# Memory's keys and half of its values projected at the start of a two-block kernel

## The chip, the cores and the metric

The kernel runs on one core of a Trainium2 chip. Its engines are TensorE (PE, with PEld for its weight loads), VectorE (DVE), ScalarE (ACT), GpSimd (POOL) and SyncE (SP); each has its own queue of instructions, and SP and POOL also issue DMA transfers. The metric is the device time of one execution in microseconds (us), less is better. Times are the median of several runs. The profile belongs to one further execution, and its span is the time inside it that the trace covers.

## The reference, cut to what matters

A first block (rmsnorm, an input projection `w_in`, a convolution, gated linear attention, a lookup over 128 x 128 experts) works on 16 meta tokens and 256 tokens of width 2048. A second block takes its 256 tokens and mixes a DeltaNet branch with cross attention to a memory. The memory's keys and values depend on inputs alone, on nothing that the first block computes:

```python
def second_block(x, mem, norm_g, mem_norm_g, mem_w_kv, ...):
    mem_n = rms_norm(mem, mem_norm_g)              # mem: 256 x 2048
    ...
        xa = memory_cross_attention(xq, mem_n, mem_w_kv[i], ...)

def memory_cross_attention(xq, mem_n, w_kv, qn_g, kn_g):
    q = rms_norm(xq.reshape(B, S, XA_HEADS, XA_DIM), qn_g)
    kv = jnp.einsum("bmd,de->bme", mem_n, w_kv)    # w_kv: 2048 x 2048
    k = rms_norm(kv[..., :XA_WIDTH].reshape(B, -1, XA_HEADS, XA_DIM), kn_g)
    v = kv[..., XA_WIDTH:].reshape(B, -1, XA_HEADS, XA_DIM)
    ...
```

The experts' output of the first block is a sum over chosen rows of a value table: `sum_k w[k] * V[idx[k]]`.

## The kernel before

Every product of fp32 matrices is made as three matmuls of parts (`mm3`, L203 to L213): an operand is cast into a `hi` part (ScalarE, L176) and a `lo` part that holds the rest (VectorE, L177), and L206, L207 and L208 multiply hi by hi, and each hi by the other's lo. Weights stream in by `load` (L185, issued on SP) as blocks of 1 MB in one of RW = 4 buffers `raw`; `halved` makes of each two halves `hi` and `lo` (HL = 4 buffers each). `proj_a` projects tokens against 512 columns: 4 loads, and for each load 24 matmuls, 96 in a block of 512 columns.

At the start SP issues `meta`, the two tiles of `x` (L111, L114) and eight small rows of gains (`prows`, L155), which TensorE turns into `prm`. Then comes the first norm: squares of the three tiles (`junk`, ScalarE L263), a row of factors made on TensorE (`along`, L297, L298), and for each of 16 slices three transposes (TensorE, L335), a product with the factors (`xs`, VectorE L337) and the split into `xh` and `xl` (L179, L180). The first projection of `w_in` follows.

The memory comes late. `memory` (a generator in `Background`, which the helpers advance by a rate at each tick) loads the memory in both layouts, makes the gain-weighted features `mh` and `ml` (L179 and L180 at its call) and the row factors `mr` (squares at L904) while TensorE works in the loop over hidden experts (L753, L754). Behind this loop stands a branch (L1141) whose body is a fallback for many chosen experts; POOL and SP wait there for a count. Behind the branch `weigh` (L1047) makes weights of pairs of experts: four gathers on POOL into `gq` and `hq` (two buffers each), their product `hq` (VectorE, L1062) and its split into `wh` and `wl` (seven buffers). Five pairs are weighed ahead (WA = 5). Then all four blocks of `w_kv` are projected (two of keys, two of values; 384 matmuls), with norms of the keys (`heads_norm`), their transposes (L318) and stores into `kmd` and `vmd`. The value loop follows: per pair of experts two gathers of 1 MB rows of V on POOL (`v_row` into `raw`), the split, 48 matmuls of 512 columns, and one `weigh` five pairs ahead, for 47 pairs.

The order of the instructions on each engine is set by a scheduler of the framework from a model of their durations; from the expert block on, that of TensorE is the order of the program.

Of the kernel before, what the change touches and what calls it, by code (L numbers as in the profile page):

```python
# [18 lines left out]
D = 2048  # L19
# [55 lines left out]
def _build(tc, nc, V, S, T, G, ctx, I, out):  # L75
# [31 lines left out]

    pn1 = ctx.enter_context(ExitStack())
    nw1 = pn1.enter_context(pool("norm1"))
    meta = nw1.tile([NM, D], F32, name="meta", bufs=1)  # L110
    nc.sync.dma_start(meta, I["meta_tokens"])  # L111
    h = hp.tile([128, 2, D], F32, name="h")
    for t in range(2):
        nc.sync.dma_start(h[:, t], I["x"][0, t * 128:(t + 1) * 128, :])  # L114
# [212 lines left out]

    w_in = I["w_in"][0]
    xh, xl = x_tiles(NM + NT)
    toks = [(meta, NM, 0), (h[:, 0], 128, NM), (h[:, 1], 128, NM + 128)]  # L330
    rB = along(nw1, rstd_of(square_sums(toks, nw1.tile([128, D], F32, name="junk")), D, [128, 3]), toks)
    for k in range(KT):
        p = (acc, ptp, acc, pmm)[k % 4]()
        for x, n, o in toks:
            T.transpose(p[:, o:o + n], chunk(x, k), ident[:n, :n])  # L335
        xs = nw1.tile([128, NM + NT], F32, name="xs", bufs=3)
        V.tensor_mul(xs, p[:, :NM + NT], rB)  # L337
        split_store(xh[:, k], xl[:, k], xs, pcol(N1, k))
# [551 lines left out]

    kmd = tc.dram_tile([128, 8, 256], F32, name="kmd")
    vmd = tc.dram_tile([128, 2, 1024], F32, name="vmd")
    def memory():

        ss = me.tile([128, 2, 4], F32, name="ssq")
        for hf in range(2):
            raw = load(I["mem_T"][:, hf * 8:hf * 8 + 8], [8, NT])
            for k in range(8):
                split_store(mh[:, hf * 8 + k], ml[:, hf * 8 + k], raw[:, k], pcol(MG, hf * 8 + k))
                yield  # L900
        for t in range(2):
            x = load(I["mem_2"][0, t * 128:(t + 1) * 128, :], [D])
            for q in range(4):
                S.activation(acc(), x[:, q * 512:(q + 1) * 512], AF.Square, accum_out=ss[:, t, q:q + 1])  # L904
            yield
        s1 = me.tile([128, 2], F32, name="ssr")
        V.tensor_reduce(s1, ss, axis=AX.X, op=OP.add)
        V.tensor_copy(mr, rstd_of(s1, D, [128, 2]))
        yield

# [210 lines left out]
    for e2 in range(NR // 2):  # L1121
        if e2 == MEM:
            pme = ctx.enter_context(ExitStack())
            me = pme.enter_context(pool("mem", side="right"))
            mh = me.tile([128, KT, NT], F32R, name="mh")
            ml = me.tile([128, KT, NT], F32R, name="ml")
            mr = me.tile([128, 2], F32, name="mr")
            bg.add(memory(), 0.75)
        for _ in hidden(e2):
            bg.tick()  # L1130
        if e2 == IX:
            bg.drain()
            index_rows()
# [16 lines left out]
    ws = [weigh(e2, wp, ww) for e2 in range(WA)]  # L1150
    wkv = I["mem_w_kv_2"][0]
    with pool("kvw", side="right") as kvw:
        ks = []
        for cb in range(2):
            for t, a in enumerate(proj_a(wkv, 0, KT, cb * 512, mh, ml)):
                ks.append(kvw.tile([128, 512], F32, name="kn", bufs=4))
                heads_norm(kvw, a, ks[-1], mr[:, t:t + 1])
        for cb in range(2):
            for t, a in enumerate(proj_a(wkv, 0, KT, 1024 + cb * 512, mh, ml)):
                vm2 = kvw.tile([128, 512], F32, name="vn")  # L1160
                S.activation(vm2, a, AF.Copy, scale=mr[:, t:t + 1])
                nc.scalar.dma_start(vmd[:, t, cb * 512:(cb + 1) * 512], vm2)
            km = kvw.tile([128, 4, 256], F32, name="kms")
            for _ in heads_T(ks[cb * 2:cb * 2 + 2], km, 0, 2):
                pass
# [613 lines left out]
```

## Time and profile before

| | us |
|---|---|
| median of 3 runs (3482.99 to 3495.45) | 3494.71 |
| the profiled execution, its own time | 3491.37 |
| its span | 3489.4 |
| TensorE busy in it | 3413.1 |

TensorE is busy for 98% of the span, at a mean granted clock of 0.995 of full speed. A row of the timeline gives start and duration in us, the engine (q behind its name for its queue of DMA issues), the line, the operation and the tiles; what stands in brackets is the engine's idle time ahead of it and what ended that. A row with `x6` joins instructions that follow each other.

### The profile page before, as it was taken

The page shows a single profiled execution, that of the slowest core. Times are in us where ns is not written, and L with a number is a line of the kernel's source. Part 1 is how long each engine was busy: PE and PEld are TensorE (multiplying, and loading weights), DVE is VectorE, ACT ScalarE, POOL GpSimd, SP SyncE. Part 2 cuts the span into 40 slices and gives each one's busy share as a digit, 9 for nine tenths or more (in the row PEclk, how much of TensorE's full clock was granted, in tenths as well). Part 3 has the DMA queues.
Part 4 walks back from the last instruction along what each step waited for, and adds up shares of the span by engine and source line. Part 5 has one row for each costly group of instructions (what it writes and reads, how often), then busy time and mean ns, then how long its engine had stood idle before and what let it go on. Part 6 is the DMA issues. An engine that isn't in the chain of part 4 may idle for free. (4 is left out here: it accounts for less than half of the span.)

```text
span 3489.4 us, 50599 instructions
## 1 busy us (share of the span) xinstructions
PE 3413.1 (98%) x19706; PEld 2968.2 (85%) x19706; DVE 2422.6 (69%) x4504; ACT 1661.4 (48%) x2276; POOL 1052.6 (30%) x660
## 2 busy tenths in 40 slices
PE   8999999999999999999998999999999999999999
PEld 7988899888889988888887788777778899999987
DVE  6975569977658998676554555444457788888775
ACT  6444443446445455455443544333347545544443
POOL 0000000000002888888841456666620000000000
PEclk9999999999999999999999999999999999999999
DMA  5544445667675677778765776666665444554443
GB/s 165 169 146 144 145 133 171 216 217 253 229 235 178 182 203 204 210 224 237 209 210 179 256 256 238 212 213 213 227 200 165 145 153 149 164 163 154 154 157 109
DMA packets 347962, 662.06 MB, mean 190 GB/s; under 512 B 56047, under 2 KB 205781, under 8 KB 318002
## 3 DMA queue, kind: packets, MB, share of 16 engines
q1 hardware_dynamic: 256962, 472.68, 40.9%
q0 software_dynamic: 71328, 165.08, 16.6%
q10 hardware_dynamic: 19424, 20.98, 1.7%
q8 instruction: 157, 2.57, 0.3%
q14 instruction: 91, 0.75, 0.1%
HBM read 620.47 MB, written 38.19 MB: 189 GB/s over the span
## 5 line engine op out<-in xcount | busy, mean ns | idle before, releaser
L176 ACT CAST hi<-raw 128x1024 fp32r<-128x1024 f32 x1093 | 1146.0, 1050 | 1510.7 <-PE acc L208 526.0
L177 DVE TENSOR_TENSOR lo<-raw,hi 128x1024 fp32r<-128x1024 f32 x1093 | 1328.0, 1221 | 646.2 <-ACT hi L176 635.4
L753 PE MATMUL acc<-xx,hi 128*128 128x512 f32 x2048 | 723.1, 398 | 0.0
L843 POOL DMA_INDIRECT table<-gts,idx x256 | 595.0, 2324 | 134.2 <-issue 75.9
L754 PE MATMUL acc<-xx,lo 128*128 128x256 f32 x2048 | 573.7, 280 | 0.0
L753 PEld LDWEIGHTS acc<-xx,hi 128*128 128x128 f32 x2048 | 384.5, 188 | 92.1
L754 PEld LDWEIGHTS acc<-xx,lo 128*128 128x128 f32 x2048 | 386.6, 189 | 0.0
L350 POOL DMA_DIRECT2D table<-zero x16 | 18.0, 1128 | 953.0 <-DVE zero L348 953.0
L206 PE MATMUL acc<-xx,hi 128*128 128x256 f32 x1024 | 304.1, 297 | 0.0
L206 PE MATMUL acc<-xh,hi 128*128 128x272 f32 (+1 forms) x1024 | 300.0, 293 | 0.7 <-DVE hg L431 0.7
L208 PE MATMUL acc<-xh,lo 128*128 128x272 f32 (+1 forms) x1024 | 297.1, 290 | 0.0
L207 PE MATMUL acc<-xl,hi 128*128 128x272 f32 (+1 forms) x1024 | 296.7, 290 | 0.0
L207 PE MATMUL acc<-xx,hi 128*128 128x256 f32 x1024 | 289.1, 282 | 0.0
L208 PE MATMUL acc<-xx,lo 128*128 128x256 f32 x1024 | 289.0, 282 | 0.0
L740 POOL DMA_INDIRECT gq<-table,ig x106 | 152.8, 1442 | 252.5 <-DVE hq L1062 116.7
L440 DVE SCALAR_TENSOR_TENSOR h<-hg,cw,h 128x256 f32<-128x256 f32 x480 | 203.4, 478 | 0.0
L1062 DVE TENSOR_TENSOR hq<-hq,gq 128x512 f32<-128x512 f32 x53 | 36.6, 691 | 234.8 <-DMA hq<-hid,ih 231.7
L206 PEld LDWEIGHTS acc<-xh,hi 128*128 128x128 f32 x1024 | 194.2, 190 | 5.2 <-issue 4.9
L207 PEld LDWEIGHTS acc<-xx,hi 128*128 128x128 f32 x1024 | 195.8, 191 | 0.2
L206 PEld LDWEIGHTS acc<-xx,hi 128*128 128x128 f32 x1024 | 195.5, 191 | 0.2
L208 PEld LDWEIGHTS acc<-xx,lo 128*128 128x128 f32 x1024 | 195.2, 191 | 0.0
L207 PEld LDWEIGHTS acc<-xl,hi 128*128 128x128 f32 x1024 | 194.1, 190 | 1.1 <-issue 1.0
(565 smaller groups left out, 6911.9 us busy)
## 6 DMA issues: line engine op xcount, KB each, us to landing
raw<-in_peer_u_dram SPq DMA_DIRECT2D x128, 1024.0 KB
raw<-in_w_in_dram SPq DMA_DIRECT2D x112, 1024.0 KB
raw<-in_dn_w_in_dram SPq DMA_DIRECT2D x88, 1024.0 KB
raw<-in_w_out_dram SPq DMA_DIRECT2D x48, 1024.0 KB
raw<-in_w_gla_out_dram SPq DMA_DIRECT2D x16, 1024.0 KB
table<-zero POOLq DMA_DIRECT2D x16, 1024.0 KB
raw<-in_w_conv_out_dram SPq DMA_DIRECT2D x16, 1024.0 KB
raw<-in_peer_wq_dram SPq DMA_DIRECT2D x16, 1024.0 KB
```

Of the source, the lines that this page charges most:

```text
L176: S.copy(hi, src)
L177: V.tensor_sub(lo, src, hi)
L206: T.matmul(o, lhsT=lh, rhs=rh, start=start, stop=False)
L207: T.matmul(o, lhsT=lh, rhs=rl, start=False, stop=False)
L208: T.matmul(o, lhsT=ll, rhs=rh, start=False, stop=stop)
L350: nc.gpsimd.dma_start(table[:128 * 128 * NT].rearrange("(q p a b) o -> q p a (b o)", q=16, p=128, b=128)[q], z[:, None, :].to_broadcast([1 ...
L440: V.scalar_tensor_tensor(ca[:, f], hg[:, f - f0, j:j + NT], w, ca[:, f], op0=OP.mult, op1=OP.add)
L740: G.indirect_dma_start(out=dst, out_offset=None, in_=rows, in_offset=bass.IndirectOffsetOnAxis(ap=ids.bitcast(U32), axis=0))
L753: T.matmul(a, lhsT=hi[:, kk], rhs=xxu[:, k].rearrange("p a t -> p (a t)"), start=k == 0, stop=False)
L754: T.matmul(a[:, :NT], lhsT=lo[:, kk], rhs=xh[:, k], start=False, stop=k == KT - 1)
L843: d = G.indirect_dma_start(out=table, out_offset=bass.IndirectOffsetOnAxis(ap=idx[:, i, s:s + 1].bitcast(U32), axis=0), in_=gts[:, i, s:s ...
L1062: V.tensor_mul(hq, hq, gq)
```

## The change

At the start, `meta` and `x` are no longer loaded by SP ahead of all else, but by POOL inside a generator `norm1`, which holds the whole first norm and runs in the background. SP's first large loads are the memory's features, rows and the first column blocks of `w_kv`. Keys 0 and 1 and values 0 (three blocks of four, 288 matmuls, 12 loads) are projected there, ahead of the first projection of `w_in`. The features and row factors are made once more in the loop over hidden experts, by two generators at rates 0.75 and 0.2 in place of one at 0.75. Behind the branch only values 1 (96 matmuls, 4 loads) is projected, and two rows of V are gathered between the second and the third `weigh`.

```diff
@@ -105,13 +105,10 @@
     OB, OL = 4, 3
 
 
+    h = hp.tile([128, 2, D], F32, name="h")
     pn1 = ctx.enter_context(ExitStack())
     nw1 = pn1.enter_context(pool("norm1"))
     meta = nw1.tile([NM, D], F32, name="meta", bufs=1)
-    nc.sync.dma_start(meta, I["meta_tokens"])
-    h = hp.tile([128, 2, D], F32, name="h")
-    for t in range(2):
-        nc.sync.dma_start(h[:, t], I["x"][0, t * 128:(t + 1) * 128, :])
 
 
     ident = cst.tile([128, 128], F32, name="ident")
@@ -325,17 +322,91 @@
         return a, b
 
 
+    kmd = tc.dram_tile([128, 8, 256], F32, name="kmd")
+    vmd = tc.dram_tile([128, 2, 1024], F32, name="vmd")
+    wkv = I["mem_w_kv_2"][0]
+
+    def mem_tiles():
+        return [me.tile([128, KT, NT], F32R, name=n) for n in ("mh", "ml")] + [me.tile([128, 2], F32, name="mr")]
+
+    def mem_features():
+
+        for hf in range(2):
+            raw = load(I["mem_T"][:, hf * 8:hf * 8 + 8], [8, NT])
+            for k in range(8):
+                split_store(mh[:, hf * 8 + k], ml[:, hf * 8 + k], raw[:, k], pcol(MG, hf * 8 + k))
+                yield
+
+    def mem_scales():
+
+        ss = me.tile([128, 2, 4], F32, name="ssq")
+        for t in range(2):
+            x = load(I["mem_2"][0, t * 128:(t + 1) * 128, :], [D])
+            for q in range(4):
+                S.activation(pmm(), x[:, q * 512:(q + 1) * 512], AF.Square, accum_out=ss[:, t, q:q + 1])
+            yield
+        s1 = me.tile([128, 2], F32, name="ssr")
+        V.tensor_reduce(s1, ss, axis=AX.X, op=OP.add)
+        V.tensor_copy(mr, rstd_of(s1, D, [128, 2]))
+        yield
+
+    def mem_keys(wk, cb):
+
+        ks = []
+        for t, a in enumerate(proj_a(wkv, 0, KT, cb * 512, mh, ml)):
+            ks.append(wk.tile([128, 512], F32, name="kn", bufs=4))
+            heads_norm(wk, a, ks[-1], mr[:, t:t + 1])
+        yield
+        km = wk.tile([128, 4, 256], F32, name="kms")
+        for _ in heads_T(ks, km, 0, 2):
+            pass
+        nc.scalar.dma_start(kmd[:, cb * 4:cb * 4 + 4], km)
+
+    def mem_values(wk, cb):
+
+        for t, a in enumerate(proj_a(wkv, 0, KT, 1024 + cb * 512, mh, ml)):
+            vm2 = wk.tile([128, 512], F32, name="vn")
+            S.activation(vm2, a, AF.Copy, scale=mr[:, t:t + 1])
+            nc.scalar.dma_start(vmd[:, t, cb * 512:(cb + 1) * 512], vm2)
+
+
     w_in = I["w_in"][0]
     xh, xl = x_tiles(NM + NT)
     toks = [(meta, NM, 0), (h[:, 0], 128, NM), (h[:, 1], 128, NM + 128)]
-    rB = along(nw1, rstd_of(square_sums(toks, nw1.tile([128, D], F32, name="junk")), D, [128, 3]), toks)
-    for k in range(KT):
-        p = (acc, ptp, acc, pmm)[k % 4]()
-        for x, n, o in toks:
-            T.transpose(p[:, o:o + n], chunk(x, k), ident[:n, :n])
-        xs = nw1.tile([128, NM + NT], F32, name="xs", bufs=3)
-        V.tensor_mul(xs, p[:, :NM + NT], rB)
-        split_store(xh[:, k], xl[:, k], xs, pcol(N1, k))
+
+    def norm1():
+        nc.gpsimd.dma_start(meta, I["meta_tokens"])
+        for t in range(2):
+            nc.gpsimd.dma_start(h[:, t], I["x"][0, t * 128:(t + 1) * 128, :])
+        yield from mem_scales()
+        rs = rstd_of(square_sums(toks, nw1.tile([128, D], F32, name="junk")), D, [128, 3])
+        yield
+        rB = along(nw1, rs, toks)
+        yield
+        for k in range(KT):
+            p = (ptp, pmm)[k % 2]()
+            for x, n, o in toks:
+                T.transpose(p[:, o:o + n], chunk(x, k), ident[:n, :n])
+            xs = nw1.tile([128, NM + NT], F32, name="xs", bufs=3)
+            V.tensor_mul(xs, p[:, :NM + NT], rB)
+            split_store(xh[:, k], xl[:, k], xs, pcol(N1, k))
+            yield
+
+
+    with pool("mem0", side="right") as me, pool("kvw0", side="right") as kvw:
+        mh, ml, mr = mem_tiles()
+        bg.add(mem_features(), 4.0)
+        bg.tick()
+        keys = [mem_keys(kvw, cb) for cb in range(2)]
+        first = bg.add(norm1(), 1.8)
+        next(keys[0])
+        next(keys[1])
+        for _ in keys[0]:
+            pass
+        mem_values(kvw, 0)
+        for _ in keys[1]:
+            pass
+        bg.drain()
     pn1.close()
 
     table = tc.dram_tile([(128 * 128 + 1) * NT, 1], F32, name="table")
@@ -887,27 +958,6 @@
         yield
         yield from compact(steps[0][:, :128])
 
-
-    kmd = tc.dram_tile([128, 8, 256], F32, name="kmd")
-    vmd = tc.dram_tile([128, 2, 1024], F32, name="vmd")
-    def memory():
-
-        ss = me.tile([128, 2, 4], F32, name="ssq")
-        for hf in range(2):
-            raw = load(I["mem_T"][:, hf * 8:hf * 8 + 8], [8, NT])
-            for k in range(8):
-                split_store(mh[:, hf * 8 + k], ml[:, hf * 8 + k], raw[:, k], pcol(MG, hf * 8 + k))
-                yield
-        for t in range(2):
-            x = load(I["mem_2"][0, t * 128:(t + 1) * 128, :], [D])
-            for q in range(4):
-                S.activation(acc(), x[:, q * 512:(q + 1) * 512], AF.Square, accum_out=ss[:, t, q:q + 1])
-            yield
-        s1 = me.tile([128, 2], F32, name="ssr")
-        V.tensor_reduce(s1, ss, axis=AX.X, op=OP.add)
-        V.tensor_copy(mr, rstd_of(s1, D, [128, 2]))
-        yield
-
     ctx.enter_context(tc.manual_schedule(engines={mybir.EngineType.PE}))
     with pool("pq") as pq:
         kT = pq.tile([128, 16, 128], F32, name="pkT")
@@ -1122,10 +1172,9 @@
         if e2 == MEM:
             pme = ctx.enter_context(ExitStack())
             me = pme.enter_context(pool("mem", side="right"))
-            mh = me.tile([128, KT, NT], F32R, name="mh")
-            ml = me.tile([128, KT, NT], F32R, name="ml")
-            mr = me.tile([128, 2], F32, name="mr")
-            bg.add(memory(), 0.75)
+            mh, ml, mr = mem_tiles()
+            bg.add(mem_features(), 0.75)
+            bg.add(mem_scales(), 0.2)
         for _ in hidden(e2):
             bg.tick()
         if e2 == IX:
@@ -1147,30 +1196,18 @@
                 for e, hi, lo in halved(load(rows, [2, 1024]), 2, 1024):
                     add_row(a, e, w, hi, lo, e == 0, e == 1)
                 take_values(a, hf)
-    ws = [weigh(e2, wp, ww) for e2 in range(WA)]
-    wkv = I["mem_w_kv_2"][0]
+    ws = [weigh(e2, wp, ww) for e2 in range(2)]
+    rows = deque(v_row(k) for k in range(2))
+    ws += [weigh(e2, wp, ww) for e2 in range(2, WA)]
     with pool("kvw", side="right") as kvw:
-        ks = []
-        for cb in range(2):
-            for t, a in enumerate(proj_a(wkv, 0, KT, cb * 512, mh, ml)):
-                ks.append(kvw.tile([128, 512], F32, name="kn", bufs=4))
-                heads_norm(kvw, a, ks[-1], mr[:, t:t + 1])
-        for cb in range(2):
-            for t, a in enumerate(proj_a(wkv, 0, KT, 1024 + cb * 512, mh, ml)):
-                vm2 = kvw.tile([128, 512], F32, name="vn")
-                S.activation(vm2, a, AF.Copy, scale=mr[:, t:t + 1])
-                nc.scalar.dma_start(vmd[:, t, cb * 512:(cb + 1) * 512], vm2)
-            km = kvw.tile([128, 4, 256], F32, name="kms")
-            for _ in heads_T(ks[cb * 2:cb * 2 + 2], km, 0, 2):
-                pass
-            nc.scalar.dma_start(kmd[:, cb * 4:cb * 4 + 4], km)
+        mem_values(kvw, 1)
     pme.close()
 
     a = [[[ptp() for _ in range(2)], [pmm() for _ in range(2)]], [[acc() for _ in range(2)] for _ in range(2)]]
     NP = NS // 2
     for e2 in range(NP - LP):
         for e in range(2):
-            for hf, hi, lo in halved(v_row(e2 * 2 + e), 2, 1024):
+            for hf, hi, lo in halved(rows.popleft() if rows else v_row(e2 * 2 + e), 2, 1024):
                 add_row(a[hf], e, ws[e2], hi, lo, e2 == 0 and e == 0, False)
             if e == 0 and e2 + WA < NP:
                 ws.append(weigh(e2 + WA, wp, ww))
```

SP at the start of the program, before: `h` is a tile of x, `prows` the gains, `raw` a block of weights.

```order
L111 DMA meta<-in_meta_tokens_dram 16x2048
L114 DMA h<-in_x_dram 128x2048 x2
L155 DMA prows<-in_norm_g_dram 16x128
L155 DMA prows<-in_conv_b_dram 16x128
L155 DMA prows<-in_conv_ln_g_dram 16x128
```

SP from the last row of gains on, after:

```order
L152 DMA prows<-in_normf_g_dram 16x128
L182 DMA raw<-in_mem_T_dram 128x2048
L182 DMA raw<-in_mem_w_kv_dram 128x4x512
L182 DMA raw<-in_mem_dram 128x2048
L182 DMA raw<-in_mem_w_kv_dram 128x4x512
L182 DMA raw<-in_mem_T_dram 128x2048
L182 DMA raw<-in_mem_dram 128x2048
L182 DMA raw<-in_mem_w_kv_dram 128x4x512 x10
L182 DMA raw<-in_w_in_dram 128x8x256 x5
L438 DMA wa<-in_w_in_dram 128x16x16
```

The loads of x have left SP, six blocks for the memory stand where they and the first blocks of `w_in` stood, and the small `wa` (a narrow weight of the first block) stands behind five blocks of `w_in` where before it stood behind six.

ScalarE at the start, before: `junk` is the square of a token tile, `hi` half a block of weights.

```order
L263 ACT_TABLE_LOAD
L263 ACTIVATE junk,ssn<-meta 16x2048
L263 ACTIVATE junk,ssn<-h 128x2048 x2
L176 CAST hi<-raw 128x1024 x4
L298 COPY rB<-mm 128x272
L179 ACTIVATE xh<-xs,prm 128x272 x16
```

ScalarE at the start, after: `mh` is a slice of the features, `mm,ssq` a quarter of a square of the memory's rows.

```order
L176 ACTIVATE mh<-raw,prm 128x256 x8
L173 CAST hi<-raw 128x1024 x2
L260 ACTIVATE junk,ssn<-meta 16x2048
L346 ACTIVATE mm,ssq<-raw 128x512 x4
L173 CAST hi<-raw 128x1024 x2
L260 ACTIVATE junk,ssn<-h 128x2048 x2
L176 ACTIVATE mh<-raw,prm 128x256 x8
L346 ACTIVATE mm,ssq<-raw 128x512 x4
L173 CAST hi<-raw 128x1024 x7
L295 COPY rB<-mm 128x272
L300 ACTIVATE kn<-acc,mr 128x512
L176 ACTIVATE xh<-xs,prm 128x272
```

The casts of the third block of `w_kv` (the first two of the seven) stand behind the squares of x, the second half of the features and the second square.

POOL behind the branch, before, from the fifth pair's gathers on (with the buffers' numbers):

```order
L740 DMA gq_24286<-table_319,ig_17496 128x256 x2
L740 DMA hq_24287<-hid_9576,ih_17499 128x256 x2
L740 DMA gq_25040<-table_319,ig_17496 128x256 x2
L740 DMA hq_25041<-hid_9576,ih_17499 128x256 x2
L740 DMA gq_25119<-table_319,ig_17496 128x256 x2
L740 DMA hq_25120<-hid_9576,ih_17499 128x256 x2
```

POOL behind the branch, after, from the second pair's last gather on:

```order
L811 DMA hq_24893<-hid_10217,ih_18138 128x256
L811 DMA raw_24901<-in_peer_v_dram,ih_18138 128x2048
L811 DMA raw_24903<-in_peer_v_dram,ih_18138 128x2048
L811 DMA gq_24907<-table_960,ig_18135 128x256 x2
L811 DMA gq_24918<-table_960,ig_18135 128x256 x2
L811 DMA hq_24908<-hid_10217,ih_18138 128x256 x2
L811 DMA hq_24919<-hid_10217,ih_18138 128x256 x2
L811 DMA raw_25170<-in_peer_v_dram,ih_18138 128x2048
L811 DMA gq_24929<-table_960,ig_18135 128x256 x2
L811 DMA raw_25215<-in_peer_v_dram,ih_18138 128x2048
```

Before, the gathers of the weights of nearly twelve pairs stand in one run, and the first row of V follows them; after, two rows of V stand behind the second pair's gathers, and further rows between those of the next pairs.

## Rows read from the trace of the kernel before

**Rows 1.** The page's first part: busy time of each engine, its share of the span, instructions.

```profile
PE 3413.1 (98%) x19706; PEld 2968.2 (85%) x19706; DVE 2422.6 (69%) x4504; ACT 1661.4 (48%) x2276; POOL 1052.6 (30%) x660
```

**Rows 2.** Waits of TensorE, whole span: us in total, times, longest us.

```profile
PE acc L207 <- DVE lo L177: 25.1, 26, 2.3
```

**Rows 3.** Stretches, start:end and length in us: busy us (instructions) of each engine, clock, DMA, GB/s.

```profile
0.00:28.50 28.50, 14.53 (x56) 9.25 (x57) 19.87 (x69) 16.20 (x22) 3.58 (x12) 1.00 0.90 309
...
1906.80:1931.90 25.10, 24.58 (x97) 19.57 (x98) 16.24 (x17) 12.66 (x16) 14.94 (x13) 0.91 0.98 365
1931.90:2003.80 71.90, 69.59 (x305) 55.64 (x303) 44.18 (x93) 39.84 (x55) 31.38 (x28) 1.00 0.73 246
2003.80:2200.00 196.20, 196.16 (x864) 162.20 (x865) 104.25 (x104) 86.16 (x92) 123.23 (x107) 1.00 0.70 241
2200.00:2525.00 325.00, 300.41 (x1279) 240.04 (x1278) 157.35 (x162) 126.52 (x134) 209.65 (x159) 0.99 0.64 216
```

**Rows 4.** Timeline of the start (start us, duration us; idle before and releaser): DMA issues and first uses.

```profile
1.19 0.89 SPq L114 DMA_DIRECT2D h<-in_x_dram  x2
...
3.15 1.08 POOL L451 DMA_DIRECT2D crow<-in_conv_w_dram  x2
...
6.17 1.12 PE L335 MATMUL acc<-ident,h 128*128 128x128 f32 x4 [1.95 <-DMA h<-in_x_dram]
...
9.41 1.12 PE L335 MATMUL acc<-ident,h 128*128 128x128 f32 x4 [2.12 <-DMA h<-in_x_dram]
...
9.79 11.89 SPq L185 DMA_DIRECT2D raw<-in_w_in_dram  x6
```

**Rows 5.** The same view: ScalarE's squares and casts, TensorE's last transposes and first projection.

```profile
6.91 1.91 ACT L263 ACTIVATE junk<-h 128x2048 f32<-128x2048 f32 x1
...
14.99 1.99 ACT L176 CAST hi<-raw 128x1024 fp32r<-128x1024 f32 x2 [3.53 <-DMA raw<-in_w_in_dram]
...
22.17 0.28 PE L335 MATMUL acc<-ident,meta 16*128 16x16 f32 x1
...
28.01 0.28 PE L335 MATMUL mm<-ident,meta 16*128 16x16 f32 x1
...
28.56 0.57 PE L206 MATMUL acc<-xh,hi 128*128 128x272 f32 x1
...
28.93 0.43 PE L207 MATMUL acc<-xl,hi 128*128 128x272 f32 x1
...
29.16 0.43 PE L208 MATMUL acc<-xh,lo 128*128 128x272 f32 x1
...
30.91 0.29 PE L207 MATMUL acc<-xl,hi 128*128 128x272 f32 x1
...
31.04 0.29 PE L208 MATMUL acc<-xh,lo 128*128 128x272 f32 x1
```

**Rows 6.** Timeline of ScalarE inside the hidden loop: Memory's features and squares of its rows.

```profile
1499.16 3.31 ACT L179 ACTIVATE mh<-raw,prm 128x256 fp32r<-128x256 f32 x8 [1.64 <-DMA raw<-in_mem_T_dram]
...
1633.49 0.58 ACT L904 ACTIVATE acc<-raw 128x512 f32<-128x512 f32 x1
```

**Rows 7.** Timeline behind the branch: load issues, and first matmuls of blocks and of the value loop.

```profile
1900.64 72.18 SPq L185 DMA_DIRECT2D raw<-in_mem_w_kv_dram  x16
...
1906.86 0.80 PE L206 MATMUL acc<-hi,mh 128*128 128x512 f32 x1 [11.98 <-ACT hi L176]
...
1931.85 0.39 PE L206 MATMUL acc<-hi,mh 128*128 128x512 f32 x1
...
2003.84 0.50 PE L206 MATMUL tp<-hi,wh 128*128 128x512 f32 x1 [0.20 <-ACT kms L319]
```

**Rows 8.** Timeline of GpSimd late in the value loop: issues of gathers into raw.

```profile
2199.55 0.94 POOL L740 DMA_INDIRECT raw<-in_peer_v_dram,ih  x1 [0.30 <-issue]
...
2206.67 1.97 POOL L740 DMA_INDIRECT raw<-in_peer_v_dram,ih  x1 [0.30 <-issue]
...
2218.58 1.96 POOL L740 DMA_INDIRECT raw<-in_peer_v_dram,ih  x1 [0.30 <-DVE lo L177]
```

## The prediction

> **What bounds the kernel now.** I read the busy times first: TensorE works 3413.1 of 3489.4 us [rows 1], so all its gaps together are 76 us, and no change that leaves its work alone can win more than that. The change moves 288 matmuls from one place to another and takes none away. What it can win lies in the gaps of two places, and I read each as a stretch.
>
> The first is the start. TensorE is busy 14.53 of 28.50 us there while the DMA engines are taken for 0.90 of the time [rows 3]: the tokens come first, then squares, factors, transposes, and only at 28.56 the first projection of w_in [rows 5]. The second is what stands behind the branch. All 16 loads of w_kv issue from 1900.64 on, and the first matmul comes at 1906.86 after 11.98 us of idleness [rows 7]. That wait is for a count and a first block of weights, and the changed kernel has both behind the branch as well. The value loop then runs full for 196 us (196.16 busy of 196.20), and from 2200 on it loses 325.00 - 300.41 = 24.6 us [rows 3]. These are nearly all of the 26 waits for VectorE's `lo`, 25.1 us in the whole span [rows 2]. So the gaps that the change can reach are 14 us at the start and 25 us in the value loop, and each has a price.
>
> **What leaves the place behind the branch.** Four blocks of w_kv are projected there. The first ends where the 97th matmul starts, 1931.85; the value loop starts at 2003.84 [rows 7]. The three blocks behind the first, with the transposes of the keys, take 72.0 us. One block stays, and it pays the cold start and the wait ahead of it as now, so 72.0 us are removed. The longer order of VectorE behind the branch (products `hq` among the parts of the four loads) could hold back a `lo` for up to 3 us, about the spare time that 16 loads' worth of cover now hides. I take 0, since the loads were issued at one every 4.5 us (72.18 / 16) [rows 7], and four buffers hold all the loads that are left.
>
> **What comes to the start.** Loads: two issues on SP took 0.89 us [rows 4], so eight rows of gains take 3.6 and the first half of the features is issued near 4.8. A tile of x of 1 MB was in use 5.0 us after its issue (1.19 to 6.17), the next 3.24 us later (9.41) [rows 4]; 3.24 us is my price of 1 MB. The features then land between 9.8 (alone) and 13.0 (with one of the two tiles of x beside them, which POOL now issues at about the same time).
>
> ScalarE: its order from there to the third block of weights is fixed. Eight features 3.31 [rows 6]; two casts of the first block 1.99 [rows 5]; the square of meta about 2.0, as for a tile of x (1.91) [rows 5]; four quarters of a square at 0.58, 2.3 [rows 6]; casts of the second block 2.0; two squares of x 3.8; eight features 3.3; four quarters 2.3; the first cast of the third block 1.0. The sum is 22.0, so that this cast ends at 32 to 35 if no input is late. Inputs are late by the transfers: ahead of that square lie two halves of features, two of x, two of the memory's rows and two blocks, 8 MB by 3.24, which from 6.6 (9.8 less one of these) is 32.5; with the square and the cast 36. A buffer is refilled only when it has been used (four `raw`), which adds to this; the ends are 33 and 43, and I take 39, nearer to the sum by transfers, as the DMA engines were taken for 0.90 at the start now [rows 3].
>
> TensorE: the first two blocks of weights give it 48 matmuls from 14.2 (9.8 + 3.31 + 1.0) at the earliest, and it has done them well ahead of 39; it waits for the third block until about 40. Then 240 matmuls are left. At 196.20 / 864 = 0.227 us each [rows 3], 0.23 with their edges, they take 55.2. The 16 slices of the first norm now stand among them. They came at (28.01 - 22.17) / 7 = 0.83 us [rows 5], but TensorE stepped slowly there: the matmuls behind them step by 0.23 (28.93 to 29.16) and two microseconds later by 0.13 (30.91 to 31.04) [rows 5]. The clock of that stretch is listed as 1.00 [rows 3]; the steps are the better witness, and I take half for a TensorE that has worked for a while: a slice at 0.42, 6.7 in all, and the 16 transposes of keys at 0.2, 3.2. They hide under no other work of TensorE, while their products and splits on VectorE and ScalarE hide beside the matmuls. The first projection of w_in starts at 40 + 55.2 + 6.7 + 3.2 = 105, with 92 and 113 as ends: 92 if the third block never holds it up (14.2 + 288 x 0.23 + 9.9, and 2 for a slow start, as the first block behind the branch has: 25.0 from 1906.86 to 1931.85, where 96 by 0.23 are 22.1 [rows 7]), 113 with the late cast (43) and 4 us of waits among keys and norm slices.
>
> Against 28.56 that is +76.4. It comes without the slow steps of today's first projection, ten by 0.1, which saves 1.0. `wa` stands behind blocks of w_in on SP, as it did; a wait for it of 0 to 2 us is possible and taken as 0, since the loads are five to six blocks ahead of its use in both orders.
>
> **What is added elsewhere.** The features and row factors are made a second time in the hidden loop, exactly the four loads and the ScalarE work that stand there now, in two generators rather than one. They are covered by the expert matmuls there, and cost nothing that is not paid now. If the later factors came after the branch, the last block's values would wait; at rate 0.2 the three steps need some fifteen ticks, and the loop is drained before the branch.
>
> **The value loop.** It starts some 72 us earlier behind the branch, with less time for POOL to gather ahead. A pair needs 48 matmuls, 10.9 us at 0.227. Two gathers into `raw` of successive pairs are 11.91 us apart in the late phase (2206.67 to 2218.58) [rows 8], so POOL's turn is 1.0 us too long, and the lead is used up after 18 pairs, near 2200. In the changed order POOL fetches rows between weights from the first; while it only issues, an issue is 0.94 us with 0.30 before it [rows 8], 6 x 1.24 = 7.4 us a pair, under 10.9. So the lead may fill as before, in which case 24.6 us stay; between a lead that is 8 pairs shorter or longer, that is 8 us either way. I take 0.
>
> **A rule that speaks against the change.** POOL's gathers show the effect of a busy VectorE: the same issue takes 0.94 us, and 1.97 and 1.96 in the phase where VectorE runs its parts back to back [rows 8]; the two loads of `crow` at the start took 1.08, 0.54 each, beside VectorE's setup [rows 4]. So the loads of meta and x lose at most 1 us each on POOL by the gathers, nothing by `crow`. The Trainium skill, page "SBUF — State Buffer", section "A bandwidth-pool intuition that's wrong (but worth ruling out)", says that a transfer whose descriptors GpSimd writes waits while VectorE holds the port that both share, and gives about 0.62 us alone and 3.1 us beside a copy. By its figure three loads would come some 7 us later and the forecast would be near 3500, an estimate; the trace's `crow` does not show it, and the later gathers show a doubling only.
>
> **The sum.** +76.4 - 72.0 - 1.0 = +3.4 on the profiled execution's 3491.37: 3494.8. This execution lies 3.3 us under the median of 3494.71, within what the runs differ by. I forecast 3495.
>
> **The rivals.** A difference of 0.5%, 17.5 us, is about what a measurement of this kernel can tell from no change: 3477 and 3512.
>
> Gains cancel (the forecast): TensorE starts early and is stopped by ScalarE's order. 3495, with a range of its own from 3487 to 3503. Chance 0.52.
>
> The start runs through: if the memory's second half is not late, the first projection starts at 92, 13 us earlier, 3482. For it speaks that ScalarE's own work is only 22 us; against it that 8 MB must land first. Chance 0.18.
>
> The change doesn't do what it says: TensorE's first projection of the memory starts no earlier than the old one did, because the gains that the features need, or the tokens of x that stand in ScalarE's order ahead of the third block, come late from POOL. At the doubled price of an issue, 1.97 for 0.94 [rows 8], three loads are 3 us late, and 5 more go if the square of x waits for its tile with all of ScalarE behind it (5.0 us from issue to use [rows 4]): 3503. The Trainium skill's page "SBUF — State Buffer", named above, is the rule for it. Chance 0.10.
>
> Slower: the cover behind the branch is too thin. POOL's turn of 11.9 us holds from the first pair when at the start of the value loop fewer than two weighed pairs and two rows are ready; then each of 47 pairs loses 1.0 us in place of 24.6 us in all, +22.4, and with +3.4 the time is 3517. For it speaks that the loop starts 25 us after the first gathers and not 97; against it that two rows are fetched ahead and an issue without waits takes 1.24. Chance 0.10.
>
> Faster: fetching rows between weights gives POOL the lead that it lacked, and the 24.6 us go: 3470. It needs the late phase to be shorter than its own lead. Chance 0.06. The rest, 0.04, lies on either side.
>
> **The numbers.** The range takes the first three and their unknown costs, 3477 to 3511, and leaves out the last two and half of the rest. Faster by over 0.5%: 0.08; within: 0.81; slower: 0.11.
>
> **What would show it.** The first matmul of w_kv near 14 to 20 and a wait of TensorE for `hi` of some 6 to 15 us before the 49th would show the ScalarE step; no such wait shows the second case. The first 272-column matmul of w_in at 105 confirms the sum at the start, at 92 refutes it. Behind the branch, the value loop should start 25 us after the first matmul. Waits for `lo` in the loop of 24.6 us, give or take 8, confirm the zero; 47 us make the slower case, none the faster one. It is wrong as a whole if the hidden loop gets longer, which I count as covered.

## The result and the profile after

The changed kernel takes 3524.25 us (median of 4 runs, 3524.03 to 3525.14) against 3494.51 us before in the same comparison: 1.0096 of it, with a 95% interval of 1.0075 to 1.0118. It is slower by 30 us, outside the range. The profiled execution has a span of 3522.0 us for 3489.4, 32.6 more.

The page's first line of the changed kernel answers to [rows 1]. TensorE does the same 19706 matmuls and is busy for 5 us more:

```profile
PE 3418.0 (97%) x19706; PEld 2965.7 (84%) x19706; DVE 2428.0 (69%) x4535; ACT 1670.7 (47%) x2308; POOL 1053.4 (30%) x663
```

The start of the changed kernel, from its timeline (start, duration, engine; idle before and releaser in brackets), answers to [rows 4] and [rows 5]:

```profile
3.62 1.09 POOL L380 DMA_DIRECT2D h<-in_x_dram  x2
9.13 0.45 PE L158 MATMUL tp<-ident,prows 128*128 128x128 f32 x1 [9.13 <-DMA prows<-in_normf_g_dram]
13.86 1.28 ACT L176 ACT_TABLE_LOAD   x1 [13.86 <-DMA raw<-in_mem_T_dram]
15.16 3.30 ACT L176 ACTIVATE mh<-raw,prm 128x256 fp32r<-128x256 f32 x8
19.45 1.22 PE L203 MATMUL acc<-hi,mh 128*128 128x512 f32 x2 [9.09 <-ACT hi L173]
...
37.15 0.74 PE L203 MATMUL acc<-hi,mh 128*128 128x512 f32 x2 [2.63 <-ACT hi L173]
...
105.22 0.37 PE L203 MATMUL acc<-xh,hi 128*128 128x272 f32 x1
```

The first projection of w_in comes at 105.22. What follows it is read from five rows of the changed kernel: the last matmul of the hidden loop, the first of w_kv, the first of the value loop, its longest wait, and its last matmul.

```profile
1971.12 0.28 PE L825 MATMUL acc<-xx,lo 128*128 128x256 f32 x1
1983.63 0.79 PE L203 MATMUL acc<-hi,mh 128*128 128x512 f32 x1 [12.24 <-ACT hi L173]
...
2009.35 0.40 PE L203 MATMUL tp<-hi,wh 128*128 128x512 f32 x1
...
2076.39 0.50 PE L204 MATMUL acc<-lo,wh 128*128 128x512 f32 x1 [4.15 <-DVE lo L174]
...
2655.40 0.39 PE L205 MATMUL acc<-hi,wl 128*128 128x512 f32 x1
```

The two that are wanted of before beside [rows 7], the end of the hidden loop and the last matmul of the value loop:

```profile
1894.59 0.28 PE L754 MATMUL acc<-xx,lo 128*128 128x256 f32 x1
...
2621.98 0.39 PE L208 MATMUL acc<-hi,wl 128*128 128x512 f32 x1
```

| stretch | before | after | difference |
|---|---|---|---|
| to the first projection of w_in | 28.56 | 105.22 | +76.7 |
| from there to the end of the hidden loop | 1866.0 | 1865.9 | -0.1 |
| to the first matmul of w_kv behind the branch | 12.3 | 12.5 | +0.2 |
| to the first matmul of the value loop | 97.0 | 25.7 | -71.3 |
| value loop, first to last matmul | 618.1 | 646.1 | +27.9 |
| the rest of the span | 867.4 | 866.6 | -0.8 |

So the move itself costs 5.5 us, and the value loop 28. TensorE's waits in the changed kernel (us in total, times, longest), beside [rows 2]:

```profile
PE acc L204 <- DVE lo L174: 42.9, 41, 4.2
...
PE tp L204 <- DVE lo L174: 5.0, 5, 1.7
```

The waits for VectorE's `lo` are 47.9 us for 25.1, 22.8 more. The rest of the 28 is TensorE's own pace behind a wait: from the first to the last matmul of the loop it is busy for 596.7 us, for 591.0 before. Stretches of the changed kernel's value loop, in the columns of [rows 3]:

```profile
2009.35:2055.00 45.65, 44.26 (x194) 35.94 (x192) 23.73 (x28) 19.60 (x23) 34.81 (x34) 1.00 0.83 292
...
2065.00:2075.00 10.00, 5.49 (x23) 3.88 (x22) 2.93 (x4) 2.52 (x3) 7.84 (x8) 1.00 0.64 196
2075.00:2085.00 10.00, 8.20 (x28) 6.28 (x29) 5.80 (x7) 4.62 (x5) 7.89 (x7) 0.83 0.55 182
...
2095.00:2205.00 110.00, 99.87 (x430) 79.79 (x429) 53.36 (x56) 42.13 (x45) 70.81 (x55) 1.00 0.63 217
2205.00:2330.00 125.00, 116.52 (x497) 93.28 (x496) 58.87 (x61) 48.78 (x52) 81.68 (x63) 0.99 0.63 213
```

Where before TensorE ran full up to 2200, here it falls behind from 2055 on, with a granted clock of 0.83 in the ten microseconds that hold the end of the 4.15 us wait (2075 to 2085), and from 2095 on it runs near the pace that before it has only after 2200.

**The start of the loop.** The first 95 us of the loop (2009.35 to 2104.35) hold the 5.0 us of waits in `tp` and these:

```profile
PE acc L204 <- DVE lo L174: 4.9, 2, 4.2
```

That makes 9.9 us, in a stretch where the kernel before waits for no `lo`. TensorE does 357 matmuls there, 81 us of work at the 0.227 us of [rows 3], so by this estimate 14 of the 28 us are lost at the start of the loop. The longest wait, which ends at 2076.39, stands behind these rows:

```profile
2071.53 0.95 POOL L811 DMA_INDIRECT hq<-hid,ih  x1 [0.30 <-issue]
```

```profile
2074.50 0.69 DVE L1112 TENSOR_TENSOR hq<-hq,gq 128x512 f32<-128x512 f32 x1 [4.74 <-DMA hq<-hid,ih]
2075.11 2.35 DVE L174 TENSOR_TENSOR lo<-raw,hi 128x1024 fp32r<-128x1024 f32 x2
```

From 2028 to 2099 GpSimd never pauses for more than 0.31 us between two issues: it fills the weight buffers, with products 6.5 to 9.2 us apart between 2044 and 2082, faster than TensorE uses them. The `lo` that TensorE needs stands on VectorE behind such a product, and the product waits for its gather.

**The ring.** Two pairs of experts in the late phase of the changed kernel. First GpSimd's issues, then VectorE:

```profile
2200.62 1.68 POOL L811 DMA_INDIRECT gq<-table,ig  x1 [2.58 <-DVE hq L1112]
2202.61 1.43 POOL L811 DMA_INDIRECT gq<-table,ig  x1 [0.30 <-issue]
2204.35 1.96 POOL L811 DMA_INDIRECT raw<-in_peer_v_dram,ih  x1 [0.30 <-issue]
2206.61 0.95 POOL L811 DMA_INDIRECT hq<-hid,ih  x1 [0.30 <-issue]
2207.86 0.95 POOL L811 DMA_INDIRECT hq<-hid,ih  x1 [0.30 <-issue]
...
2213.21 1.68 POOL L811 DMA_INDIRECT gq<-table,ig  x1 [3.15 <-DVE hq L1112]
```

```profile
2199.66 0.69 DVE L1112 TENSOR_TENSOR hq<-hq,gq 128x512 f32<-128x512 f32 x1 [6.17 <-DMA hq<-hid,ih]
2200.27 2.35 DVE L174 TENSOR_TENSOR lo<-raw,hi 128x1024 fp32r<-128x1024 f32 x2
2202.54 0.69 DVE L174 TENSOR_TENSOR wl<-hq,wh 128x512 fp32r<-128x512 f32 x1
2203.14 2.36 DVE L174 TENSOR_TENSOR lo<-raw,hi 128x1024 fp32r<-128x1024 f32 x2
2212.25 0.69 DVE L1112 TENSOR_TENSOR hq<-hq,gq 128x512 f32<-128x512 f32 x1 [6.75 <-DMA hq<-hid,ih]
```

The product of a pair ends at 2200.35. GpSimd, which waits for it, issues two gathers of `gq` for the pair after the next and a row of V, and only then, 6.3 us later, the two of `hq` for the next pair. They land 3.4 us after their last issue, and VectorE has stood still for them for 6.75 us with the `lo` of the value rows queued behind the product. Product, free buffer, gather, product: once round is 12.6 us here and 12.2 on average between 2200 and 2500, for 10.9 us of matmuls. The queue order shows why: GpSimd fetches `gq` of one pair ahead of `hq` of the pair before it (numbers after the names are tiles; the pair's two tiles have successive numbers).

```
L811 DMA gq_26470<-table_960,ig_18135 128x256 x2
L811 DMA raw_26276<-in_peer_v_dram,ih_18138 128x2048
L811 DMA hq_26392<-hid_10217,ih_18138 128x256 x2
```

`gq` is free when the product has read it; the product stands in `hq`, which is free only when the split has read it, and the split of the pair before stands behind the product on VectorE (its cast waits for a free weight buffer, that is, for TensorE). So the two gathers of one pair go out a turn apart, and the second has only half a turn left.

### The profile page after: what moved, and what is told of

Read it like the earlier page. It is cut to its first block, busy times and chain, and to the rows that moved or that the text cites. A ratio compares the mean times of both kernels' runs of the same rounds, so it can differ in the third digit from the quotient of the medians.

```text
span 3522.0 us, 50645 instructions
## 1 busy us (share of the span) xinstructions
PE 3418.0 (97%) x19706; PEld 2965.7 (84%) x19706; DVE 2428.0 (69%) x4535; ACT 1670.7 (47%) x2308; POOL 1053.4 (30%) x663
## 5 line engine op out<-in xcount | busy, mean ns | idle before, releaser
L914 POOL DMA_INDIRECT table<-gts,idx x256 | 586.6, 2291 | 134.4 <-issue 75.9
L204 PE MATMUL acc<-lo,wh 128*128 128x512 f32 x424 | 171.5, 405 | 41.9 <-DVE lo L174 41.5
```

Of the source, the lines that this page charges most:

```text
L204: T.matmul(o, lhsT=lh, rhs=rl, start=False, stop=False)
L914: d = G.indirect_dma_start(out=table, out_offset=bass.IndirectOffsetOnAxis(ap=idx[:, i, s:s + 1].bitcast(U32), axis=0), in_=gts[:, i, s:s ...
```

## The experiments

**Is it the cover or the order of the fetches?** The changed kernel, without rows of V between the weights:

```diff
-    ws = [weigh(e2, wp, ww) for e2 in range(2)]
-    rows = deque(v_row(k) for k in range(2))
-    ws += [weigh(e2, wp, ww) for e2 in range(2, WA)]
+    ws = [weigh(e2, wp, ww) for e2 in range(WA)]
...
-            for hf, hi, lo in halved(rows.popleft() if rows else v_row(e2 * 2 + e), 2, 1024):
+            for hf, hi, lo in halved(v_row(e2 * 2 + e), 2, 1024):
```

> The changed kernel without the two rows of V gathered ahead: behind the branch five pairs are weighed first, as before, and only values 1 is projected there. Theory A (the cover behind the branch is too thin: with 26 us of matmuls in place of 97 the weights' ring of gather, product and split never gets a lead, so every pair takes about 12 us for 10.9 us of matmuls): waits for lo in the value loop stay at 40 to 50 us, span 3515 to 3525. Theory B (the rows gathered between the weights hold up the weights): waits fall to about 25 us, span near 3500.

3521.89 us, ratio 1.011 (1.0061 to 1.0159), span 3520.4. The waits for `lo` are 34.1 us, less than expected, but one more of 6.8 us stands at the start of the loop (for the copy `vn`, which ScalarE does late in this order), and the loop takes 643 us for the 646 of the change. The rows fetched ahead do not make the loss.

And the kernel before with its cover cut, nothing moved to the start:

```diff
-        ks = []
-        for cb in range(2):
-            for t, a in enumerate(proj_a(wkv, 0, KT, cb * 512, mh, ml)):
...
+        for t, a in enumerate(proj_a(wkv, 0, KT, 1024 + 512, mh, ml)):
+            vm2 = kvw.tile([128, 512], F32, name="vn")
+            S.activation(vm2, a, AF.Copy, scale=mr[:, t:t + 1])
+            for cb in range(2):
+                nc.scalar.dma_start(vmd[:, t, cb * 512:(cb + 1) * 512], vm2)
+                nc.scalar.dma_start(kmd[:, cb * 4 + t * 2:cb * 4 + t * 2 + 2], vm2)
```

> The kernel before with three of the four blocks of the memory left out (both of keys and the first of values; nothing is computed in their place, and what is left is stored where they stood), so that the start and the hidden loop are as before and only the cover behind the branch is as thin as after the change. Theory A: the 72 us of the blocks go and some 20 to 27 us come back as waits for lo, span 3437 to 3444. Theory B, or one that puts the loss at the start or in the hidden loop: the waits stay at 25 us and the span is 3417.

3446.12 us, ratio 0.9889 (0.9842 to 0.9936), span 3445.2. Three blocks, 72 us, are gone, and the span is only 44 us shorter. TensorE's waits in it:

```profile
PE acc L207 <- DVE lo L177: 33.5, 36, 3.7
...
PE acc L206 <- ACT vn L1155: 9.7, 1, 9.7
```

The value loop takes 645.8 us (1932.84 to 2578.67), the length of the changed kernel's. So a loss comes with thin cover alone, with the start and the hidden loop as before. That its size is the same is in part luck: 9.7 us of waits are for `vn`, which the changed kernel does not have, and those for `lo` are 33.5 us and not 47.9. The span is 1 us over the expected.

The dose between, with the first values behind the branch as well:

```diff
-        mem_values(kvw0, 0)
...
-        mem_values(kvw, 1)
+        for cb in range(2):
+            mem_values(kvw, cb)
```

> The changed kernel with both blocks of values behind the branch, and only the keys at the start. Theory A by dose (the lead grows with the matmuls behind the branch, and the loop pays about 1 us for every pair after the lead is used up): twice the cover of the change, waits between 47 and 24.6, near 38 us, span 3510 to 3517. If only the prefetched rows or the start matter: as after, 3522.

3507.38 us, ratio 1.0038 (1.0024 to 1.0052), span 3505.2; 32.3 us of waits for `lo`, and a loop of 625.1 us (2013.59 to 2638.65). It lies between one block (646) and four (618), nearer to four than I expected: the second block gives back 21 us, the third and the fourth together 7. In its first 95 us the loop has a single wait, of 5.7 us for `lo`; behind them the waits are 24.8 us, as the 24.6 of the kernel before, where the changed kernel has 36.6.

**What closes the ring?** A third buffer for `hq`, in either kernel:

```diff
-        hq = ww.tile([128, 2, NT], F32, name="hq")
+        hq = ww.tile([128, 2, NT], F32, name="hq", bufs=3)
```

> The changed kernel with three buffers of hq in place of two (2 KB more a partition). If what closes the ring is hq's buffer (the next hidden row is gathered only when the split of the pair before has read its own, and the product waits for that row with the parts of V behind it on VectorE), waits for lo in the value loop fall from 47 to under 15 us, span 3485 to 3490. If the ring is closed by the gathers' issue times or by gq, they stay over 40, span 3515 to 3525.

> The kernel before with three buffers of hq. If hq's buffer closes the ring: waits for lo in the value loop fall from 24.6 to under 8 us, span 3466 to 3473. If not: unchanged, 3489.

The first: 3523.38 us, ratio 1.0109 (1.0061 to 1.0157). The second: 3486.04 us, 0.9995 (0.9974 to 1.0015). The waits for `lo` are 34.7 us in the first, which neither guess had, with 6.1 for `vn`, and 20.5 in the second. My guess fell: a buffer more changes nothing that these runs can tell. VectorE's wait from 2200 to 2500 is the same in the changed kernel and with the third buffer, here in this order:

```profile
DVE hq L1112 <- DMA hq<-hid,ih: 159.0, 25, 7.7
```

```profile
DVE hq L1112 <- DMA hq<-hid,ih: 155.7, 25, 7.7
```

The products run one pair further ahead, and the buffers are full one pair later: a pair's weights still wait for TensorE to free a weight buffer, the split behind the product still holds `hq`, and `hq` is still fetched behind `gq` of the pair after it. What had to go was the holding, not the count. So the product got a tile of its own:

```diff
-        V.tensor_mul(hq, hq, gq)
-        split_store(wh, wl, hq)
+        pq = ww.tile([128, 2, NT], F32, name="pq", bufs=1)
+        V.tensor_mul(pq, hq, gq)
+        split_store(wh, wl, pq)
```

> The changed kernel with the product of the two gathered tiles written into a tile of its own (2 KB a partition), so that the gathered tiles come free with the product and not with the split, which waits for a free weight of a pair seven earlier. Theory A in its second form (the ring is product, free buffer, gather, product: the next hidden row is fetched only after the product before it, behind three other gathers, and VectorE waits for it with the parts of V behind): the gathers then have a whole pair's time and the waits for lo fall from 47 us to under 10, span 3480 to 3488. If GpSimd's issues or the transfers themselves set the 12 us a pair, the waits stay over 35 us and the span over 3510.

> The kernel before with the same tile for the product. Theory A: the 24.6 us of waits for lo go, span 3465 to 3470. If issues or transfers set the pace: 3489.

In the changed kernel 3474.28 us, ratio 0.9947 (0.993 to 0.9964), 50 us less than without it; in the kernel before 3457.19 us, ratio 0.9895 (0.9878 to 0.9911). GpSimd in the changed kernel with the tile, then VectorE:

```profile
2253.95 1.69 POOL L811 DMA_INDIRECT gq<-table,ig  x1 [1.71 <-DVE pq L1113]
2255.94 1.74 POOL L811 DMA_INDIRECT hq<-hid,ih  x1 [0.31 <-issue]
2257.99 0.95 POOL L811 DMA_INDIRECT gq<-table,ig  x1 [0.30 <-issue]
2259.24 1.16 POOL L811 DMA_INDIRECT hq<-hid,ih  x1 [0.30 <-issue]
...
2264.82 1.69 POOL L811 DMA_INDIRECT gq<-table,ig  x1 [1.71 <-DVE pq L1113]
```

```profile
2252.99 0.69 DVE L1113 TENSOR_TENSOR pq<-hq,gq 128x512 f32<-128x512 f32 x1
2253.59 1.22 DVE L174 TENSOR_TENSOR lo<-raw,hi 128x1024 fp32r<-128x1024 f32 x1
...
2263.86 0.69 DVE L1113 TENSOR_TENSOR pq<-hq,gq 128x512 f32<-128x512 f32 x1
```

Both gathers of a pair now go out together, right after a product, and have a whole turn to land. The product waits for no transfer, and turns are 10.87 us apart, the pace of the matmuls. Issues still take up to 1.74 us and GpSimd has 1.7 us to spare, so with the ring open slow issues, which I had blamed, don't set the pace. In the closed ring they are part of the round: in the kernel before, the issues from the first `gq` to the last `hq` take 7.2 us of a turn of 11.2 at 2088.66 and 8.2 of 11.9 at 2202.94. With the tile in the kernel before the waits for `lo` are

```profile
PE acc L207 <- DVE lo L177: 3.0, 2, 2.5
```

and none of them lies in its loop, which takes 580.9 us (2009.65 to 2590.53). The expected span was 3465 to 3470 and 3457.1 was measured, since the slow matmuls behind the waits went as well: 37.2 us of loop for 24.6 us of waits, with TensorE busy for 578.4 us in place of 591.0.

The tile does not give back all that the change lost. In the changed kernel the loop takes 595.0 us with it (2010.46 to 2605.49), 14.1 more than in the kernel before with it. TensorE's waits for `lo` in the whole span are

```profile
PE tp L204 <- DVE lo L174: 5.6, 3, 3.2
PE acc L204 <- DVE lo L174: 4.4, 2, 4.1
```

and all of them in the loop, 9.7 us, lie in its first 95 us.

So the loss at the start of the loop does not come from the held tile. That it comes from GpSimd, which issues there without a pause as in the changed kernel, is read from the trace; no run changed it.

Two controls, both in the kernel before. The product over `gq` in place of `hq`, which swaps the tile that is held:

```diff
-        V.tensor_mul(hq, hq, gq)
-        split_store(wh, wl, hq)
+        V.tensor_mul(gq, hq, gq)
+        split_store(wh, wl, gq)
```

> The kernel before with the product written over gq in place of hq: no more memory, the roles of the two gathered tiles swapped. If the ring is closed because one of the two tiles is held from the product to the split (whichever it is), the other's role changes nothing: the value loop keeps its 20 to 25 us of waits, span 3483 to 3490, and VectorE's product now waits for gq. If it is closed by hidden rows (hq) alone, the waits go and the span is near 3460.

3488.08 us, ratio 0.9998 (0.9981 to 1.0015); the profiled execution is 3479.5, a little under the expected. VectorE now waits for the other tile, 2200 to 2500:

```profile
DVE gq L1062 <- DMA gq<-table,ig: 145.6, 25, 7.7
```

And two buffers of the product's tile, which lets the products run as far ahead as before:

```diff
-        pq = ww.tile([128, 2, NT], F32, name="pq", bufs=1)
+        pq = ww.tile([128, 2, NT], F32, name="pq", bufs=2)
```

> The kernel before with two buffers for the product's own tile. The product then runs one pair further ahead, as far as in the kernel before, but both gathered tiles are free with it. If freeing the gathered tiles is what opens the ring: as with one buffer, span 3453 to 3460. If it was the product's later place on VectorE: the waits come back in part, 3470 to 3490.

3453.58 us, ratio 0.9902 (0.9866 to 0.9939), with 0.5 us of waits for `lo`. Not the product's place on VectorE but the free gathered tiles open the ring.

**The start.** The changed kernel with the tokens on SP:

```diff
-        nc.gpsimd.dma_start(meta, I["meta_tokens"])
+        nc.sync.dma_start(meta, I["meta_tokens"])
         for t in range(2):
-            nc.gpsimd.dma_start(h[:, t], I["x"][0, t * 128:(t + 1) * 128, :])
+            nc.sync.dma_start(h[:, t], I["x"][0, t * 128:(t + 1) * 128, :])
```

> The changed kernel with meta and x loaded on SP, behind the first features and the first block of w_kv, in place of GpSimd's queue. If the loads on GpSimd's queue share the transfers with the features and hold them back, the first slice of the features (13.86 us after the change) comes 2 to 5 us earlier, near 10 us, and the first matmul with it; the third block is then set by the tokens and the first projection of w_in stays between 100 and 106. If they don't, the first features land within 1 us of 13.86.

One execution, 3522.46 us. Its timeline:

```profile
9.75 1.28 ACT L176 ACT_TABLE_LOAD   x1 [9.75 <-DMA raw<-in_mem_T_dram]
```

```profile
5.71 0.45 PE L158 MATMUL tp<-ident,prows 128*128 128x128 f32 x1 [5.71 <-DMA prows<-in_normf_g_dram]
```

The features land 4.1 us earlier (9.75 for 13.86), the gains 3.4 us, and the first projection of w_in stands at 101.25 for 105.22. The 4 us hardly show in the span, 3520.6 for 3522.0: the value loop takes 648.7 us here for 646.1. With the product's tile as well:

> The changed kernel with the product's own tile and with x loaded on SP: the best of the start's orders tried with the open ring. The first w_in projection came at 101.25 with x on SP and at 105.22 without; if the two gains add, span 3467 to 3469, which still stays 10 us over the kernel before with the product's tile; if they don't, 3472.

3464.73 us, ratio 0.9937 (0.9919 to 0.9955). The first projection is at 99.84 in it, and its profiled execution (3458.8, under the 3467 to 3469 that I expected) also passes from there to the end of the hidden loop in 1858.0 us where both kernels of the case take 1866. No wait of TensorE accounts for these 8 us. Its matmuls follow each other faster (1156 in the 200 us from 1699.84 for 1134 in the same stretch of the changed kernel, both at a granted clock of 1.00), and why is not shown. The ratios with x on SP and without, 0.9937 and 0.9947, do not tell the two apart. The kernel before with the product's tile, 3457.19 or 3453.58 us, beats this and both kernels of the case: with the ring open, the change still costs 17 us (3474.28 for 3457.19), and the spans, 15.0 us apart, place 14.1 of them in the value loop.

## Why the prediction was wrong

**The start** was right in its sum, by luck. The first projection was forecast at 105 and came at 105.22, but errors cancelled. The features landed at 13.86, beyond my 9.8 to 13.0, and ScalarE then loaded a table for 1.28 us that I had not counted, so TensorE started at 19.45 and not at 14.2. In return it was held up by the third block for 2.63 us only, not 6 to 15, since the late and slow first 48 matmuls filled the time; that block came at 37.15 where I had 40. ScalarE waited for no input from 13.86 until then: 13.86, the table and the 22.0 us that I had summed for it make 37.1, so the sum by transfers, to which I had leaned, did not bind. What followed took 68.1 us for my 65.1, with a wait of 0.74 us and a granted clock of 0.51 from 39.6 to 42.3 behind it.

**Behind the branch** 72.0 us were to go, and 71.3 went. **The hidden loop** was to pay nothing for the second set of features: 1865.9 us for 1866.0.

**The rule of the page "SBUF — State Buffer"** (the Trainium skill, section "A bandwidth-pool intuition that's wrong (but worth ruling out)") would have the loads of meta and x held back by VectorE, if VectorE's short setup instructions act as the copy that it names. The trace shows no such delay: the two issues of x took 1.09 us together beside VectorE's setup. What the loads did was to share the transfers: with x on SP behind the first features these land 4.1 us earlier, in one execution. In the value loop the issues beside VectorE's back-to-back parts, which are no copies, do take 1.4 to 2.0 us for 0.95, in the direction of the rule, at well under the fivefold of its figure.

**The value loop** is the step that failed: I took 0, with 8 us either way, and it was +27.9. The zero rested on GpSimd filling its lead between the rows of V as the long cover had let it, and two things came in its place, by the estimate above about 14 us each. At the start of the loop GpSimd had no time to spare: it issued without a pause until 2099, and TensorE waited 9.9 us for `lo` that stood behind products. I had taken the time of its issues, 7.4 us a pair, against 10.9, and not how late the first gathers would land with the loop already running. Then the ring took over, from 2101 on, 92 us into the loop, where before it did so from 2166 on, 162 us into it: 36.6 us of waits for 24.6.

I had listed what happened as the slower rival ("the cover behind the branch is too thin"), priced at +22.4 and 3517, with a chance of 0.10. The added waits are 22.8 us, 21.9 of them in the loop, and 5.6 came on top by the slower matmuls behind them, which no term had. That the price fits the waits is partly luck: the turn of 11.9 us does not hold from the first pair, and the loss at the start of the loop was not in it.

The reason I gave against it was wrong as well: I read the 11.9 us between two issues as GpSimd's own time, found 7.4 us of issues when nothing else slows them, and took the lead as sure to fill. In the late phase GpSimd was not short of time. It waited for VectorE's product and VectorE for GpSimd's gather, and such a ring has no lead to regain: in the kernel before it went round in 11.1 us on average from 2044 to 2166 and in 12.2 from there to 2519, both longer than the 10.9 us of matmuls. The long cover put its loss off for 18 pairs. What shows it was in the trace before, though not among my rows (2200 to 2500, GpSimd and VectorE):

```profile
POOL gq L740 <- DVE hq L1062: 68.9, 25, 4.1
```

```profile
DVE hq L1062 <- DMA hq<-hid,ih: 159.3, 25, 7.7
```

GpSimd's wait ahead of every turn named VectorE's product, and VectorE's wait named GpSimd's gather. I read the issues and not the waits ahead of them.

## What to carry to other kernels

When two engines each wait for the other in turn, price the ring by one full round, from a release back to the same release, and compare it with the work that it feeds; if the round is longer, work ahead of the loop only delays the loss, and taking that cover away brings it forward. A tile that a gather fills should be freed by the first instruction that reads it: computing in place ties the next gather to the whole chain behind, and one more buffer did not untie it here. A move that costs little by itself can still lose what the moved work had covered, so ask of every block that leaves a place what ran under it: here the lead of the ring, and the filling of the buffers, which cost 14 us even with the ring open.

## What the runs showed of the hardware

In the late phase of both kernels the issue of one gather on GpSimd takes about 0.95 us, and 1.4 to 2.0 us beside VectorE's back-to-back parts, three of the six in a turn. With the ring open up to 1.74 us remain in the rows shown, and TensorE waits for none of them there. Behind a wait of a few microseconds TensorE's matmuls stay slow for a while: 28 of them in 10 us at a granted clock of 0.83 around the end of a wait of 4.15 us. So a microsecond of waiting in the loop cost 1.3 to 1.5 in all (27.9 for the 21.9 that the change added, 37.2 for the 24.6 that the tile took away in the kernel before). A transfer of 2 MB on GpSimd's queue delayed one of 1 MB that SP issued 0.8 us later by 4.1 us (13.86 for 9.75, one execution each). One of 13 runs of the kernel before took 3460.29 us, about its time with the ring open, and others lie between 3473.66 and 3497.40; there is no trace of the fast ones, so that their lead lasted by chance is only argued.
